# The second pass of the attention's scores with a stationary operand of 128 rows

## The chip, the cores and the metric

The kernel runs on one core of a Trainium2 chip. The metric is the device time of one execution in microseconds. The engines named below are TensorE (PE; its weight loads are listed apart as PEld), VectorE (DVE), ScalarE (ACT), GpSimd (POOL) and SyncE (SP), which issues the transfers.

## The reference

One layer of a decoder trunk over 2048 tokens of width 1024, all in float32: a normalised input is projected for three groups of heads (a state-space group, a gated linear recurrence, and an attention with forget gates), their outputs are projected back, a gated feed-forward of width 2816 follows, and then a gated embedding term. The change touches the attention alone. For one head with queries q and keys k of 64 elements, and cum, the running sum of the logarithms of the forget gates, the reference computes

```python
logits = jnp.einsum("bqhe,bkhe->bhqk", q[:, q0:q1], k[:, :q1]).astype(jnp.float32) * scale
logits = logits + cum[:, :, q0:q1, None] - cum[:, :, None, :q1]
mask = (q0 + jnp.arange(Q_BLOCK))[:, None] >= jnp.arange(q1)[None, :]
logits = jnp.where(mask[None, None], logits, -jnp.inf)
probs = jax.nn.softmax(logits, axis=-1).astype(v.dtype)
outs.append(jnp.einsum("bhqk,bkhe->bqhe", probs, v[:, :q1]))
```

There are 6 such heads.

## The kernel before

TensorE multiplies in a format (fp32r) that holds fewer bits than float32. So every factor x is split into a high part, which is x rounded to that format, and a low part, which is the rest. A product is made of three passes into one bank of the accumulator: high x high, high x low, low x high (lines 190 to 192 for all projections, each with 128 rows of contraction and 512 tokens).

The tokens go in 4 blocks of 512. Phase 1 projects the input and writes q, k and v to DRAM in both parts; phase 1b holds the state-space group, with the attention of token block 0 among it; phase 3 holds the feed-forward of each token block, with the attention of the next block put in small pieces between the products (`Side.tick`, called from `mm3`). The attention of block qc handles one head after another: `scores(h)` is a run of pieces, each one query block of 128 (line 560, `qi`) against up to 512 keys (line 568, `kc`), and `outputs(h)` transposes the probabilities and multiplies them with the values (lines 602 to 608). A tile scheduler sets the final order of the instructions on each engine from priorities and a timeline model; on the chip each engine then works through its list in that order.

For the scores a head has 64 elements, so both parts of a factor fit into 128 partitions. `qx` holds the high part of q in partitions 0 to 63 and the low part in 64 to 127; `kx` holds the low part of k in 0 to 63 and the high part in 64 to 127. One pass of 128 rows (line 571) thus gives q high x k low + q low x k high. The second pass (line 572) gives q high x k high: for it `qh` repeats the high part of q in partitions 64 to 127, where the high part of k lies, and both operands are the upper 64 partitions alone.

The tiles `qx`, `kx`, `qh` and `cum` have one buffer each. The transfers for the next head are issued from SP's queue once the last score of a head has read them. The scores go to four accumulator banks in turn (`xa`, `xe`, `xb`, `xc`). DVE adds the running sums and takes the row's maximum on the way out (line 576); ACT applies the exponential (line 583); DVE divides by the row's sum (line 586).

Of the kernel before, what the change touches and what calls it, by code (L numbers as in the profile page):

```python
# [19 lines left out]
P = 128  # L20
# [12 lines left out]

# columns of the packed parameters, one value per partition
PC = {}
# [5 lines left out]
NPC = _n  # L41
NALL = PC["scw"]  # of these the first are used all along


class Side:
    """work put in small pieces between the products of the main line"""

# [17 lines left out]
class Trunk:  # L65
# [17 lines left out]

    # ---------------------------------------------------------------- pieces
    def consts(self):
# [14 lines left out]
    def softplus(self, x, n):  # L100
        """log(1 + exp(x)) on a small tile, log1p by its atanh series (argument at most 1/3)."""
        nc, p = self.nc, self.spool
# [27 lines left out]
    def rms(self, ssq, n, tag="xc"):  # L130
        """1/sqrt(mean + eps) of every token, on all partitions (PSUM)."""
        nc = self.nc
        ms = self.ps(tag, (P, NCH))
        for c in range(NCH):
            nc.tensor.matmul(ms[:, c:c + 1], lhsT=ssq[:, c * P:(c + 1) * P], rhs=self.ones[:, 0:1], start=True, stop=True)
        v = self.t(self.small, [P, NCH], "rv")
        nc.vector.tensor_scalar(v, ms, 1.0 / n, EPS, op0=ALU.mult, op1=ALU.add)
        r = self.t(self.small, [P, NCH], "rr")
        nc.gpsimd.tensor_tensor(r, v, self.mhalf, op=ALU.pow)
        rh = self.t(self.small, [P, NCH], "rh", F32R)  # L140
        nc.vector.tensor_copy(rh, r)
        rl = self.t(self.small, [P, NCH], "rl")
        nc.vector.tensor_tensor(rl, r, rh.bitcast(F32), op=ALU.subtract)
        rb = self.ps(tag)
        for i, x in enumerate((rh.bitcast(F32), rl)):
            dg = self.t(self.tmp, [P, TB], "sq", F32R, bufs=3)
            nc.vector.tensor_tensor(dg.rearrange("p (a b) -> p a b", a=NCH), self.ident.unsqueeze(1).to_broadcast([P, NCH, P]),
                                    x.unsqueeze(2).to_broadcast([P, NCH, P]), op=ALU.mult)
            nc.tensor.matmul(rb, lhsT=self.onesr, rhs=dg, start=i == 0, stop=i == 1)
        return rb  # L150
# [13 lines left out]
    def split(self, hi, lo, x, g):  # L164
        """hi + lo = x * g in two tiles of the tensor engine's precision."""
        nc = self.nc
# [6 lines left out]
    def weight(self, src, nk):  # L173
        """A block of weights from DRAM in two parts, hi and lo: [P, 2, nk, P]."""
        nc = self.nc
# [7 lines left out]
    def mm3(self, w, u, rate=0):  # L183
        """w^T u in three passes; u: list of [P, 2, TB]; rate: pieces of the side work to put between"""
        nc = self.nc
# [10 lines left out]
    def parts(self, k, x, eng):  # L196
        """x as hi + lo"""
        nc = self.nc
# [5 lines left out]
    def norm_split(self, h, g, inplace=False, eng=None, tag="mm"):  # L204
        """RMSNorm of h [P, KD, TB] with gain, as a list of hi/lo tiles"""
        nc = self.nc
# [8 lines left out]
    def norm_store(self, blocks, n, row, tb, tag="xc"):  # L215
        """normalised (gain still missing) blocks of the mixer's output to DRAM"""
        nc = self.nc
# [6 lines left out]

    # ---------------------------------------------------------------- phase 1
    def load_norm(self, tb, xp):
# [9 lines left out]
    def phase1(self, ctx):  # L236
        """norm, v, forget gates and steps, LRU, q, k"""
        nc, tc, a = self.nc, self.tc, self.a
# [4 lines left out]
        u_next = self.load_norm(0, one)  # L243
        # block diagonal weights of the LRU gates
        self.load_mpar(one)
# [26 lines left out]
        for tb in range(NTB):  # L272
# [5 lines left out]
            if tb == 0:  # L278
                # weights of v, f and dt stay
                wv = self.t(one, [P, 2, KD, 396], "wv", F32R)  # L280
# [9 lines left out]
    def qk(self, nm, b, tb, u, two):  # L290
        """two heads of q (scaled) or k, in two parts, to DRAM"""
        nc = self.nc
# [8 lines left out]
    def values(self, tb, u, wv, sgn, mul, two):  # L301
        """v of the attention, f and dt, token-major; running sums of log f and of a dt within chunks"""
        nc = self.nc
# [33 lines left out]
    def lru(self, tb, u, wa, halo, hba, msp, carry, two):  # L337
# [16 lines left out]
        for b in range(2):  # L354
            tg = []
            for g in range(2):
# [4 lines left out]
                tg.append(th)  # L361
            # t = tanh(log(a) / 2), expm1(log a) = 2 t / (1 - t)
            tt = tg[0]
# [19 lines left out]
    def phase1b(self, ctx):  # L383
        """SSD"""
        nc, tc, a = self.nc, self.tc, self.a
# [11 lines left out]
        for tb in range(NTB):  # L397
# [13 lines left out]
            if tb == NTB - 1:  # L411
                # the first tokens of the next phase
                yx = self.load_y(0)
# [15 lines left out]
    def conv(self, wsrc, u, halo, cw, cb, two, dst, silu):  # L429
        """projection of one block of channels, causal convolution over 4 tokens; with silu the taps come halved"""  # L430
        nc = self.nc
# [16 lines left out]
    def ssd_chunk(self, tb, c, xbc, small, state, ys, two):  # L448
# [5 lines left out]
        acol = small[:, 1, c]  # L454
        # running sums along the chunk on all partitions
        ab = self.t(two, [P, 6, P], "ab")
        nc.sync.dma_start(ab, self.drow[tb, c * 12 + 6:c * 12 + 12].partition_broadcast(P))
        # token-major x and B
        ptr = self.ps("xa", (P, 3, P))
# [8 lines left out]
        nc.scalar.activation(bt, pgb[:, 2:4], ACT.Copy)  # L468
        # decays: of the whole chunk, to its end, from its start
        ex = self.t(two, [P, 3, 6], "ex")  # L470
# [9 lines left out]
        nc.scalar.activation(seg, seg, ACT.Exp)  # L480
        # x * dt, and the same decayed to the end of the chunk
        px = ptr.rearrange("p j (i e) -> p (j i) e", i=2)
# [4 lines left out]
        for g in range(2):  # L487
            nc.vector.tensor_tensor(seg[:, 3 * g:3 * g + 3], seg[:, 3 * g:3 * g + 3],
                                    pgb[:, g].unsqueeze(1).to_broadcast([P, 3, P]), op=ALU.mult)
        # token-major y from the state before the chunk and from the chunk itself  # L490
        yt = self.t(two, [P, 6, 64], "yt", bufs=1)
        if not first:
# [3 lines left out]
            nc.vector.tensor_tensor(yt, pso, ex[:, 2].unsqueeze(2).to_broadcast([P, 6, 64]), op=ALU.mult)  # L496
        # state at the end of the chunk
        pst = self.ps("xa", (P, 6, 64))
# [21 lines left out]

    # ---------------------------------------------------------------- phase 2
    def att_setup(self):
        """negated running sums of log f over all tokens, one head per partition; the mask of a diagonal block"""
        nc = self.nc
# [13 lines left out]
    def attention(self, qc, pool, tags, tag_o):  # L538
        """forgetting attention of one block of queries; a generator that yields between small pieces"""
        nc = self.nc  # L540
# [5 lines left out]
        def scores(h):  # L546
# [6 lines left out]
            for s in range(2):  # L553
                nc.sync.dma_start(qx[64 * s:64 * s + 64].bitcast(F32), q[:, s])
                nc.sync.dma_start(kx[64 - 64 * s:128 - 64 * s].bitcast(F32).rearrange("p a b -> p (a b)"), k[:, s])
            nc.sync.dma_start(qh[64:128].bitcast(F32), q[:, 0])
            nc.sync.dma_start(cum.rearrange("p a b -> p (a b)"), self.dcum[h, 0:n * TB].partition_broadcast(P))
            probs = []
            for qi in range(NCH):
# [7 lines left out]
                for kc in range(n):  # L567
# [3 lines left out]
                    nc.tensor.matmul(ps[:, :w], lhsT=qx[:, qs], rhs=kx[:, kc, :w], start=True, stop=False)  # L571
                    nc.tensor.matmul(ps[:, :w], lhsT=qh[64:128, qs], rhs=kx[64:128, kc, :w], start=False, stop=True)  # L572
                    d = w - P if k1 == W else w
# [47 lines left out]

    # ---------------------------------------------------------------- phase 3
    def load(self, src):
# [4 lines left out]
    def load_y(self, tb):  # L628
        """the mixer's output with gains; the rest of the attention's part is done before it is normalised here"""
        nc = self.nc  # L630
# [15 lines left out]
    def mix(self, tb, c, yx):  # L646
        """a block of columns of the mixer's projection and the residual"""
        x = self.load(self.a["xt"][c, :, tb * TB:(tb + 1) * TB])
# [5 lines left out]
    def phase3(self, ctx):  # L654
# [10 lines left out]
        for tb in range(NTB):  # L665
# [3 lines left out]
            if more:  # L669
                side.start(self.attention(tb + 1, one, ("xa", "xe", "xb", "xc"), "xd"))  # L670
                # pieces of attention for each block of columns
                rate = 6 * (8 * (tb + 2) + 1) / RATE
# [18 lines left out]
            u = self.norm_split(h, "g3", eng=V, tag="xe")  # L691
            # the embedding's projection
            px = self.t(one, [P, 4, TB], "kx", F32R)
# [9 lines left out]
            for c in range(KD):  # L703
# [3 lines left out]
                nc.scalar.activation(em[c], ps, ACT.Copy)  # L707
            # the gate, among the first products of the next tokens
            hn = []
# [43 lines left out]
def layout(inp):  # L753
    f = {k: np.asarray(v) for k, v in inp.items()}
    A = np.ascontiguousarray

    def blocks(w):  # [K, C] -> [C/128, 128 (k inner), K/128, 128 (c)]
        k, c = w.shape
        return A(w.reshape(k // P, P, c // P, P).transpose(2, 1, 0, 3))

    def cols(v):  # [n*128] -> [128, n]
        return v.reshape(-1, P).T
# [47 lines left out]
```

## Time and profile before

| what | value |
|---|---|
| median of 3 runs | 3008.57 us (3006.9 to 3009.61) |
| span of the profiled execution | 3008.8 us |
| PE busy | 2902.0 us (96%) |
| DVE, ACT, POOL busy | 1755.2, 1175.0, 1211.1 us |
| first score pass, line 571 | 240 matmuls |
| second score pass, line 572 | 240 matmuls |
| three passes of the projections, lines 190 to 192 | 1306.9, 1294.3, 1292.9 us busy |

Busy time of TensorE is the union of modelled spans that overlap: a matmul of 512 columns is listed with some 400 ns, and the next one starts before it ends. What a matmul occupies of the engine is read from the distance between starts. The profiled execution lies within 0.3 us of the median of the runs, so its numbers can be used for the runs as they stand.

### The profile page before, as it was taken

The numbers are of one execution on the slowest core, as the hardware profiler recorded it, in microseconds if no ns is written. First come the engines' busy times: TensorE is split into PE (matmuls) and PEld (weight loads), VectorE is DVE, ScalarE is ACT, GpSimd is POOL, SyncE is SP. The second block draws the span as 40 slices with busy tenths as digits, with TensorE's granted clock in tenths as the row PEclk, the third lists the DMA queues.
The fourth block names the chain that finished last, engine by engine and source line by source line (L and its number), as shares of the span: only waits on it lengthen the run. The fifth ranks groups of instructions, "written<-read, shape, count | busy, mean of one in ns | idle before, by whom it ended". The sixth has DMA issues, their size and how long they took to land.

```text
span 3008.8 us, 34985 instructions
## 1 busy us (share of the span) xinstructions
PE 2902.0 (96%) x12981; PEld 2307.3 (77%) x12981; DVE 1755.2 (58%) x3001; ACT 1175.0 (39%) x1751; POOL 1211.1 (40%) x635
## 2 busy tenths in 40 slices
PE   6998899999999999999999999999999999999997
PEld 5777677777877778877777788777777888788885
DVE  7888768988654533646555446564564464623246
ACT  5454434443343333434333334343343343322233
POOL 5444555333433334443233344433223344444442
PEclk9999999998999999999999999999999999999998
DMA  5444444343433333433343334243333243332331
GB/s 181 167 160 155 158 144 151 115 153 108 154 119 107 124 101 108 144 109 124 111 132 100 120 108 145 84 145 105 113 117 109 71 127 123 113 98 94 101 96 67
DMA packets 154301, 365.46 MB, mean 121 GB/s; under 512 B 17260, under 2 KB 48652, under 8 KB 152588
## 3 DMA queue, kind: packets, MB, share of 16 engines
q1 hardware_dynamic: 154130, 363.21, 37.3%
q8 instruction: 103, 1.69, 0.2%
q14 instruction: 68, 0.56, 0.1%
HBM read 318.87 MB, written 44.29 MB: 121 GB/s over the span
## 4 chain that ended last, share of the span: by engine, by line
PE 75%; DVE 14%; DMA 3%; ACT 3%; issue 3%; POOL 1%; SPq 0%; POOLq 0%; DVEq 0%; ACTq 0%
PE mm L190 21%; PE mm L191 21%; PE mm L192 21%; PE xd L608 1%; PE xd L607 1%; DVE xbc L440 1%; DVE h L440 1%; DVE u L201 1%; DMA ld<-dy 1%; DVE seg L479 1%; PE xa L602 1%; PE xa L572 1%; PE xb L572 1%; PE xe L602 1%; POOL w L180 1%
## 5 line engine op out<-in xcount | busy, mean ns | idle before, releaser
L180 POOL TENSOR_TENSOR w<-wst,w 128x1024 fp32r<-128x1024 f32 (+1 forms) x424 | 1029.4, 2429 | 1437.6 <-ACT w L179 1353.5
L190 PE MATMUL mm<-u,w 128*128 128x512 f32 x3264 | 1306.9, 402 | 11.9 <-ACT u L200 7.8
L191 PE MATMUL mm<-u,w 128*128 128x512 f32 x3264 | 1294.3, 397 | 11.9 <-DVE u L201 11.8
L192 PE MATMUL mm<-u,w 128*128 128x512 f32 x3264 | 1292.9, 397 | 0.5 <-POOL w L180 0.5
L190 PEld LDWEIGHTS mm<-u,w 128*128 128x128 f32 x3264 | 618.4, 190 | 159.0 <-issue 21.5
L191 PEld LDWEIGHTS mm<-u,w 128*128 128x128 f32 x3264 | 619.2, 190 | 145.1 <-DVE u L201 16.4
L192 PEld LDWEIGHTS mm<-u,w 128*128 128x128 f32 x3264 | 618.7, 190 | 134.4 <-issue 8.2
L179 ACT ACTIVATE w<-wst 128x1024 fp32r<-128x1024 f32 (+1 forms) x424 | 440.4, 1040 | 549.6 <-PE mm L192 354.3
L684 DVE SCALAR_TENSOR_TENSOR u<-th,u 128x512 fp32r<-128x512 f32 x88 | 187.8, 2134 | 59.8 <-ACT u L683 59.5
L583 ACT ACTIVATE lg<-lg,m 128x128 f32<-128x128 f32 (+7 forms) x96 | 115.4, 1202 | 181.7 <-DVE m L581 175.1
L161 DVE TENSOR_TENSOR ssq<-ssq,sq 128x512 f32<-128x512 f32 x111 | 133.6, 1203 | 57.2 <-ACT sq L157 55.2
L681 DVE TENSOR_TENSOR th<-th,mm 128x512 f32<-128x512 f32 x88 | 60.3, 685 | 172.0 <-PE mm L192 171.3
L690 DVE TENSOR_TENSOR h<-h,mm 128x512 f32<-128x512 f32 x96 | 65.5, 685 | 133.8 <-PE mm L192 133.3
L679 ACT ACTIVATE th<-mm 128x512 f32<-128x512 f32 x88 | 52.6, 597 | 228.9 <-PE mm L192 228.7
L563 POOL TENSOR_TENSOR cd<-cum,maskT 128x128 f32<-128x128 f32 x96 | 47.6, 496 | 202.9 <-DVE mx L576 117.6
L680 DVE SCALAR_TENSOR_TENSOR th<-th,mm 128x512 f32<-128x512 f32 x88 | 60.2, 685 | 117.6 <-ACT th L679 117.6
L718 DVE SCALAR_TENSOR_TENSOR th<-th,lg 128x512 f32<-128x512 f32 x32 | 31.0, 968 | 111.4 <-ACT th L717 111.3
L586 DVE TENSOR_SCALAR lg<-lg,r 128x128 f32<-128x128 f32 (+7 forms) x96 | 94.1, 981 | 2.6
L608 PE MATMUL xd<-ph,vc 128*128 128x512 f32 x216 | 83.6, 390 | 0.0
L607 PE MATMUL xd<-ph,vc 128*128 128x512 f32 x216 | 81.0, 375 | 0.0
L606 DVE TENSOR_TENSOR ph<-xa,ph 128x512 fp32r<-128x512 f32 x54 | 37.2, 688 | 50.9 <-ACT ph L605 50.7
L606 DVE TENSOR_TENSOR ph<-xc,ph 128x512 fp32r<-128x512 f32 (+1 forms) x66 | 36.6, 555 | 47.3 <-ACT ph L605 47.3
(293 smaller groups left out, 3228.8 us busy)
## 6 DMA issues: line engine op xcount, KB each, us to landing
wst<-in_w_gate SPq DMA_DIRECT2D x88, 512.0 KB, 3.5
wst<-in_w_up SPq DMA_DIRECT2D x88, 512.0 KB, 3.5
wst<-in_w_down SPq DMA_DIRECT2D x64, 448.0 KB, 3.3
wst<-in_w_out SPq DMA_DIRECT2D x32, 512.0 KB, 3.6
wst<-in_w_down SPq DMA_DIRECT2D x32, 512.0 KB, 3.5
wst<-in_w_pg SPq DMA_DIRECT2D x32, 512.0 KB, 3.5
vc<-dv SPq DMA_DIRECT2D x60, 256.0 KB, 3.6
wst<-in_w_xbc SPq DMA_DIRECT2D x28, 512.0 KB, 3.5
```

The costliest lines, as they stand in the source:

```text
L161: (eng or nc.gpsimd).tensor_tensor(acc, acc, s, op=ALU.add)
L179: nc.scalar.activation(w[:, 0], st, ACT.Copy)
L180: nc.gpsimd.tensor_tensor(w[:, 1], st, w[:, 0].bitcast(F32), op=ALU.subtract)
L190: nc.tensor.matmul(ps, lhsT=w[:, 0, k], rhs=x[:, 0], start=k == 0, stop=False)
L191: nc.tensor.matmul(ps, lhsT=w[:, 0, k], rhs=x[:, 1], start=False, stop=False)
L192: nc.tensor.matmul(ps, lhsT=w[:, 1, k], rhs=x[:, 0], start=False, stop=k == n - 1)
L583: nc.scalar.activation(lg, lg, ACT.Exp, bias=m, scale=1.0, accum_out=l)
L586: nc.vector.tensor_scalar(lg, lg, r, None, op0=ALU.mult)
L606: nc.vector.tensor_tensor(ph[:, 1, sl], pt[:, sl], ph[:, 0, sl].bitcast(F32), op=ALU.subtract)
L607: nc.tensor.matmul(po[:, sl], lhsT=vc[:, kt], rhs=ph[:, 0, sl], start=kt == 0, stop=False)
L608: nc.tensor.matmul(po[:, sl], lhsT=vc[:, kt], rhs=ph[:, 1, sl], start=False, stop=kt == nkt - 1)
L684: nc.vector.scalar_tensor_tensor(hh[:, 1], th, 0.5, hh[:, 0].bitcast(F32), op0=ALU.mult, op1=ALU.subtract)
```

## The change

`qh` gets all 128 partitions: the high part of q in 64 to 127, as before, and now the low part in 0 to 63. The second pass multiplies the whole of `qh` with the whole of `kx` and so gives q high x k high + q low x k low. The fourth product of the parts, low x low, which was left out before, comes with it. For this there is one more transfer of 64 partitions per head. Comments and documentation lines are dropped as well (not shown); since one line is added, lines from 557 on have a number higher by one.

```diff
-            nc.sync.dma_start(qh[64:128].bitcast(F32), q[:, 0])
+            for s in range(2):
+                nc.sync.dma_start(qh[64 - 64 * s:128 - 64 * s].bitcast(F32), q[:, s])
...
                     nc.tensor.matmul(ps[:, :w], lhsT=qx[:, qs], rhs=kx[:, kc, :w], start=True, stop=False)
-                    nc.tensor.matmul(ps[:, :w], lhsT=qh[64:128, qs], rhs=kx[64:128, kc, :w], start=False, stop=True)
+                    nc.tensor.matmul(ps[:, :w], lhsT=qh[:, qs], rhs=kx[:, kc, :w], start=False, stop=True)
```

The scheduler's lists for the two kernels are the same but for a few places. On SP's queue, this is the start of a head of token block 3 before (dq, dk, dcum and dv are the scratch tensors in DRAM, wst the staging of a weight block):

```order
L554 DMA qx_11599<-dq_81 64x512
L555 DMA kx_11597<-dk_82 64x1536
L554 DMA qx_11599<-dq_81 64x512
L555 DMA kx_11597<-dk_82 64x1536
L556 DMA qh_11600<-dq_81 64x512
L557 DMA cum_11598<-dcum_88 128x1536
L177 DMA wst_11881<-in_w_gate 128x1024
```

and now:

```order
L554 DMA qx_11612<-dq_81 64x512
L555 DMA kx_11610<-dk_82 64x1536
L554 DMA qx_11612<-dq_81 64x512
L555 DMA kx_11610<-dk_82 64x1536
L557 DMA qh_11613<-dq_81 64x512 x2
L558 DMA cum_11611<-dcum_88 128x1536
L177 DMA wst_11895<-in_w_gate 128x1024
```

The second transfer into `qh` stands right behind the first; `cum` and all that follows is one place further back. It is the same at each of the 24 heads.

On TensorE the order differs by more than a place or two only in phase 1b, around the last heads of token block 0. There the end of one head's outputs (xe) and the first scores of the next head (xc, xd) stood here before (mm are the products of a projection):

```order
L608 MATMUL xe_4826<-ph_4882,vc_4824 128x256
L607 MATMUL xe_4826<-ph_4898,vc_4824 128x128
L608 MATMUL xe_4826<-ph_4898,vc_4824 128x128
L571 MATMUL xc_4954<-kx_4940,qx_4942 128x128
L572 MATMUL xc_4954<-kx_4940,qh_4943 128x128
L571 MATMUL xd_4978<-kx_4940,qx_4942 128x256
L572 MATMUL xd_4978<-kx_4940,qh_4943 128x256
L190 MATMUL mm_5906<-u_1237_5770,w_5903 128x512
```

and now stand here:

```order
L190 MATMUL mm_5954<-u_1237_5776,w_5951 128x512
L191 MATMUL mm_5954<-u_1237_5776,w_5951 128x512
L609 MATMUL xe_4831<-ph_4887,vc_4829 128x256
L608 MATMUL xe_4831<-ph_4903,vc_4829 128x128
L609 MATMUL xe_4831<-ph_4903,vc_4829 128x128
L572 MATMUL xc_4960<-kx_4945,qx_4947 128x128
L573 MATMUL xc_4960<-kx_4945,qh_4948 128x128
L572 MATMUL xd_4984<-kx_4945,qx_4947 128x256
L573 MATMUL xd_4984<-kx_4945,qh_4948 128x256
L516 MATMUL xb_5431<-ident_91,yt_5412 128x128 x3
```

They have moved behind most of the next projection (mm_5954 is the one that follows mm_5912, the old mm_5906), some 20 products later in TensorE's list. In phase 3 the difference is a handful of single places.

## The prediction

> **What bounds the kernel now.** I read the page first (its busy times and its chain), then the busy times by stretch, then the matmuls one by one where the changed line stands.
>
> ```profile
> span 3008.8 us, 34985 instructions
> PE 2902.0 (96%) x12981; PEld 2307.3 (77%) x12981; DVE 1755.2 (58%) x3001; ACT 1175.0 (39%) x1751; POOL 1211.1 (40%) x635
> PE 75%; DVE 14%; DMA 3%; ACT 3%; issue 3%; POOL 1%; SPq 0%; POOLq 0%; DVEq 0%; ACTq 0%
> ...
> L192 PE MATMUL mm<-u,w 128*128 128x512 f32 x3264 | 1292.9, 397 | 0.5 <-POOL w L180 0.5
> ```
>
> TensorE is busy nearly all the time and makes up three quarters of the chain that ended last. The last row shows that weights are never late: the third pass waited for GpSimd's low parts for 0.5 us in the whole run. By stretch (the first two are the phases ahead of the feed-forward, the next three hold the attention of token blocks 1 to 3, the last has no attention):
>
> ```profile
> 400.00:670.00 270.00, 254.33 (x1238) 202.97 (x1238) 230.59 (x515) 119.79 (x220) 127.05 (x85) 0.99 0.45 145
> 670.00:1240.00 570.00, 561.42 (x2537) 447.32 (x2536) 311.69 (x580) 207.41 (x319) 219.31 (x119) 0.99 0.37 119
> 1240.00:1830.00 590.00, 586.63 (x2609) 457.80 (x2608) 312.16 (x542) 229.81 (x328) 221.58 (x115) 1.00 0.37 118
> 1830.00:2410.00 580.00, 578.88 (x2564) 443.39 (x2564) 311.64 (x575) 228.42 (x316) 199.66 (x103) 0.99 0.35 109
> 2410.00:3009.00 599.00, 574.92 (x2523) 472.58 (x2521) 269.36 (x288) 194.42 (x260) 251.53 (x110) 0.98 0.31 102
> ```
>
> Columns are stretch, length, then busy time of PE, weight loads, DVE, ACT, POOL, then granted clock, DMA share, GB/s. From 670 to 2410 us TensorE idles 8.6 + 3.4 + 1.1 = 13 us in 1740, while DVE is at 54%. So whatever time a matmul gives up there comes off the end. From 400 to 670 us DVE is at 85% and TensorE at 94%: two engines share the bound.
>
> But a busy TensorE need not be streaming. The group by line for the second score pass (64 rows) shows that something holds it:
>
> ```profile
> L572 PE MATMUL xa<-kx,qh x54: 439/497/503, 824.0 to 2331.0; 64*128 64x512 f32 x48, 64*128 64x384 f32 x6
> ...
>   issue: 69.6, 215
> ```
>
> Its weight loads follow 69.6 us of idle load time in 215 places, in which nothing was waited for. What that is, the matmuls in order of time show (start, duration; durations overlap, so starts are what to subtract):
>
> ```profile
> 1984.16 0.40 PE L571 MATMUL xa<-kx,qx 128*128 128x512 f32 x1
> 1984.49 0.50 PE L572 MATMUL xa<-kx,qh 64*128 64x512 f32 x1
> 1984.91 0.50 PE L190 MATMUL mm<-u,w 128*128 128x512 f32 x1
> 1985.25 0.40 PE L571 MATMUL xe<-kx,qx 128*128 128x512 f32 x1
> 1985.58 0.49 PE L572 MATMUL xe<-kx,qh 64*128 64x512 f32 x1
> 1986.00 0.50 PE L191 MATMUL mm<-u,w 128*128 128x512 f32 x1
> 1986.34 0.40 PE L571 MATMUL xc<-kx,qx 128*128 128x512 f32 x1
> 1986.66 0.50 PE L572 MATMUL xc<-kx,qh 64*128 64x512 f32 x1
> 1987.09 0.50 PE L192 MATMUL mm<-u,w 128*128 128x512 f32 x1
> 1987.43 0.40 PE L190 MATMUL mm<-u,w 128*128 128x512 f32 x1
> 1987.66 0.39 PE L191 MATMUL mm<-u,w 128*128 128x512 f32 x1
> ...
> 1989.95 0.40 PE L571 MATMUL xb<-kx,qx 128*128 128x512 f32 x1
> ```
>
> Two full-row matmuls follow each other at 1987.66 - 1987.43 = 0.23 us. Around a 64-row one the steps are 0.33 (1984.16 to 1984.49), 0.42 and 0.34, that is 1.09 us for three matmuls in place of 0.69. **Each 64-row pass costs 0.40 us beyond a full-row one.** The weight loads say why:
>
> ```profile
> 1984.48 0.18 PEld L572 LDWEIGHTS xa<-kx,qh 64*128 64x128 f32 x1 [0.37 <-issue]
> 1984.91 0.19 PEld L190 LDWEIGHTS mm<-u,w 128*128 128x128 f32 x1 [0.25 <-issue]
> 1985.02 0.19 PEld L571 LDWEIGHTS xe<-kx,qx 128*128 128x128 f32 x1
> ```
>
> The load for 1985.25 starts at 1985.02, a matmul ahead of its use. The load of the 64-row operand starts only with its own matmul (1984.48 and 1984.49), and so does the load of the full-row operand behind it (1984.91). Twice per pair a load of about 0.19 us is not hidden, which is 0.38 of the 0.40.
>
> **The change part by part.** (1) The second pass gets 128 rows. It streams the same columns (0.23 us for 512), its load is as long (0.18 against 0.19), and there is no other shape left beside it. Line 572 is the one score pass of 64 rows; by the loops it runs 6 heads x 4 query blocks x (1 + 2 + 3 + 4) = 240 times, 24 of them ahead of 670 us and 216 behind. Of each head's pieces in token block qc, 4 qc + 1 are 512 wide and one each is 384, 256 and 128 wide, so of the 216 there are 162 of full width and 54 narrower. For the narrowest I take this place:
>
> ```profile
> 1387.48 0.22 PE L571 MATMUL xb<-kx,qx 128*128 128x128 f32 x1
> 1387.63 0.32 PE L572 MATMUL xb<-kx,qh 64*128 64x128 f32 x1
> ...
> 1388.22 0.40 PE L192 MATMUL mm<-u,w 128*128 128x512 f32 x1
> ```
>
> From 1387.48 to 1388.22 are 0.74 us for two narrow and one wide matmul. Full-row, the wide one takes 0.23; for each narrow one the bounds are a quarter of that (0.06) and a load's length (0.19), so the excess lies between 0.74 - 0.61 = 0.13 and 0.74 - 0.35 = 0.39. I take 0.3. For 384 and 256 columns, which lie between, I take 0.38. Sum behind 670 us: 162 x 0.40 + 18 x 0.38 x 2 + 18 x 0.3 = 64.8 + 13.7 + 5.4 = 84 us. TensorE is the bound there, so I count all but 3 us of it, for waits that today's slower pace covers: 81 us.
>
> Ahead of 670 us stand 24 pieces, 6 of each width: 6 x (0.40 + 0.38 + 0.38 + 0.3) = 9 us. With DVE at 85% there, it may be worth between 9 and, as the order of the attention's products among those of the state-space part moves by some 20 products, a loss of 5. I take the middle of 0 and 9, 5 us with rounding.
>
> (2) What uncovers after that? A score's bank must be free before its next use, and DVE frees it:
>
> ```profile
> 1983.47 0.69 DVE L576 CUSTOM_DVE_ANT_0 lg<-xb,cum 128x512 f32<-128x512 f32 x1 [1.18 <-PE xb L572]
> ...
> 1985.02 0.69 DVE L576 CUSTOM_DVE_ANT_0 lg<-xa,cum 128x512 f32<-128x512 f32 x1 [0.67 <-PE xa L572]
> 1985.64 0.08 DVE L576 DVE_READ_ACCUMULATOR2_ANT mx<- 128x1 f32 x1
> ...
> 1989.69 0.69 DVE L681 TENSOR_TENSOR th<-th,mm 128x512 f32<-128x512 f32 x1 [0.45 <-PE mm L192]
> ```
>
> Bank xb is read out by 1984.16 and written next at 1989.95, 5.8 us later; and DVE waits for TensorE (0.67 us), not the other way. That covers the 0.4 us by which a piece gets shorter.
>
> (3) One more transfer per head, 24 in all, of 64 partitions (128 KB). It stands on SP's queue right behind the first transfer into qh; behind it wait the running sums (cum), then weight blocks and values.
>
> ```profile
> 817.51 0.59 SPq L556 DMA_DIRECT2D qh<-dq  x1
> ...
> 1998.27 0.59 SPq L556 DMA_DIRECT2D qh<-dq  x1
> ...
> DMA to landing us min/median/max: 2.9/5.3/8.9
> ```
>
> ```profile
> 824.00 0.50 PE L572 MATMUL xa<-kx,qh 64*128 64x512 f32 x1
> ...
> 2033.70 0.50 PE L572 MATMUL xa<-kx,qh 64*128 64x512 f32 x1
> ```
>
> An issue takes 0.59 us. In the usual case (1998.27) the operand is used 35 us later, while the head before is multiplied with its values; the second transfer lands in 0.59 + 8.9 us at most. Only the first head of block 1 is tight: issue 817.51, use 824.00, 6.5 us, and 0.59 + 5.3 = 5.9 just fits. Cost: 0, and 24 x 0.59 = 14 us if that cover were gone at every head. DVE, ACT and POOL get no instruction more.
>
> **Sum**, against the profiled execution: 3008.8 - 81 - 5 = 2923 us. Its span is within 0.3 us of the median of the runs (3008.57), so nothing is added: **2923 us**.
>
> **The rivals.** *DVE paces the bursts.* Pieces come in bursts of about four. After the change one takes 0.69 us of TensorE against 0.69 + 0.08 - overlap, about 0.70 us, of DVE (1985.02 to 1985.72). If a main-line operation (0.69, line 681) falls into each burst and the bank's cover is used up, 216 / 4 x 0.69 = 37 us come back: 2960 us. Against it: the 5.8 us of cover and a DVE at 54%. I give it 10%.
>
> *The rows are not the reason.* The load of 64 rows takes 0.18 us against 0.19, so by duration alone nothing is gained, and it would be 3009 us, no change. The trace speaks against it: loads start late around this shape and nowhere else in the bursts. I give it 3%. The Trainium skill ("TensorE: Matmul & The Clock Gate", LDWEIGHTS (loading the stationary operand)) says that a load's time goes by columns and that the row count doesn't matter; by that rule alone the sum would be this rival's. The rows 0.18 and 0.19 agree with it, but it says nothing of when the load may start. The skill's "TensorEngine Tiling (Array Packing)", Key Properties, says that a change of tiling mode drains the engine; by that rule the sum is my own.
>
> *Slower: the head starts late.* With qh landing after the head's turn, TensorE stands at line 573 with the main line's products queued behind it. It decides from 86 / 24 = 3.6 us per head on; with the issue and the longest landing fully exposed, 0.59 + 8.9 = 9.5 us, it would be 3009 - 86 + 24 x 9.5 = 3151 us. At 35 us of cover in the usual head I give it 2%. A fall of the granted clock would have to reach 5% (86 of 1740 us), and the last stretch, all full-row passes, has 0.98.
>
> **How the numbers follow.** My forecast has 83%, the three rivals 10, 3 and 2, and 2% go to gains beyond the range. Low end: all 84 and 9 us and some luck of the new order, 2910. High end: the early phase loses 5 instead of gaining, 10 us less, and half of the DVE rival's 37 us come back, 2951. This kernel's measurement tells some 0.2% (6 us) from no change. Faster: 83 + 10 + 2 = 95%; within: 3%; slower: 2%.
>
> **What would show it.** Right: steps of 0.23 us between lines 572, 573 (the old 571, 572) and the next matmul; loads of line 573 a matmul ahead, its idle "issue" time near 0; TensorE's weight loads unchanged in number; the stretch with 96 pieces shorter by about 37 us, and the last stretch unchanged. Wrong: the steps stay at 0.33 and 0.42 (the second rival); idle time before lines 572 or 190 released by DVE (the first); or by a landing of qh or cum (the third).

## The result, and the profile after

The changed kernel takes 2930.56 us (median of 4 runs, 2927.95 to 2933.44) against 3009.09 us beside it: a ratio of 0.9738 with a 95% interval of 0.9724 to 0.9752, 78.5 us less. Forecast were 2923 us, 2910 to 2951.

The page of the changed kernel, its totals and its chain of waits:

```profile
span 2926.6 us, 35034 instructions
PE 2812.5 (96%) x12981; PEld 2317.3 (79%) x12981; DVE 1751.9 (60%) x3001; ACT 1175.7 (40%) x1751; POOL 1213.2 (41%) x635
...
PE 72%; DVE 3%; issue 1%; DMA 1%; ACT 1%; POOL 0%; POOLq 0%; DVEq 0%; ACTq 0%
```

The numbers of matmuls and weight loads are as before, and so is the work of the other engines. TensorE's busy time fell by 89.5 us, the span by 82.2. (The shares of the chain add up to 78% here and to 99% before, so they can't be compared one by one.) By stretch (columns as before; the bounds lie where the same work starts and ends now, about):

```profile
400.00:670.00 270.00, 252.42 (x1253) 206.57 (x1253) 230.97 (x511) 121.21 (x221) 126.26 (x85) 0.98 0.46 148
670.00:1220.00 550.00, 539.21 (x2512) 445.42 (x2511) 310.04 (x584) 206.09 (x318) 218.69 (x119) 0.98 0.39 124
1220.00:1780.00 560.00, 555.65 (x2594) 458.34 (x2593) 310.53 (x540) 227.34 (x325) 220.84 (x114) 1.00 0.39 125
1780.00:2330.00 550.00, 546.69 (x2607) 452.37 (x2606) 310.61 (x577) 231.84 (x322) 204.59 (x104) 1.00 0.38 119
2330.00:2927.00 597.00, 572.62 (x2506) 470.80 (x2504) 268.27 (x287) 193.86 (x260) 250.46 (x109) 0.98 0.30 102
```

In the three stretches with attention TensorE still has few gaps (18 us in 1660, where it was 13 in 1740), and VectorE is at 56%. The second score pass (now line 573), by line, and in order of time in a burst of the last attention block:

```profile
L573 PE MATMUL xa<-kx,qh x54: 335/392/403, 824.5 to 2248.5; 128*128 128x512 f32 x48, 128*128 128x384 f32 x6
```

```profile
1929.40 0.40 PE L190 MATMUL mm<-u,w 128*128 128x512 f32 x1
1929.64 0.39 PE L572 MATMUL xa<-kx,qx 128*128 128x512 f32 x1
1929.87 0.40 PE L573 MATMUL xa<-kx,qh 128*128 128x512 f32 x1
1930.10 0.39 PE L191 MATMUL mm<-u,w 128*128 128x512 f32 x1
1930.33 0.40 PE L572 MATMUL xe<-kx,qx 128*128 128x512 f32 x1
```

```profile
1929.40 0.19 PEld L572 LDWEIGHTS xa<-kx,qx 128*128 128x128 f32 x1
1929.64 0.19 PEld L573 LDWEIGHTS xa<-kx,qh 128*128 128x128 f32 x1
1929.87 0.19 PEld L191 LDWEIGHTS mm<-u,w 128*128 128x128 f32 x1
```

Every step is 0.23 us now; from one first pass to the next (1929.64 to 1930.33) it is 0.69 us, where it was 1.09. Each load starts a matmul ahead of its use, and the idle time under "issue" is gone from the line's group. The whole trace says the same: before, 239 of the 240 loads for the second pass start no more than 2 ns ahead of their matmul, and the loads for the matmuls behind them no more than 3 ns; now the median load for the second pass starts 227 ns ahead.

Where in the program did the time go? One instruction, the same in all traces (the 3015th matmul), serves as a mark near the end of the early phases: a matmul of line 192 right behind a state-space chunk's transposes of line 466. All 24 pieces of block 0 lie ahead of it and all others behind it. It stands here before

```profile
733.13 0.48 PE L192 MATMUL mm<-u,w 128*128 128x512 f32 x1
```

and here after

```profile
733.32 0.48 PE L192 MATMUL mm<-u,w 128*128 128x512 f32 x1
```

Up to this mark nothing was gained. Behind it, 3008.8 - 733.1 = 2275.7 us became 2926.6 - 733.3 = 2193.3 us: the whole 82 us. The two stretches behind the mark, before and after (columns as above):

```profile
733.13:3008.80 2275.67, 2246.12 (x9970) 1775.40 (x9968) 1148.09 (x1854) 832.88 (x1173) 876.37 (x435) 0.99 0.35 113
```

```profile
733.32:2926.60 2193.28, 2160.81 (x9970) 1783.04 (x9968) 1142.46 (x1854) 833.10 (x1173) 877.71 (x435) 0.99 0.37 118
```

TensorE's busy time fell by 85.3 us there, and its idle time rose by 2.9 us (29.6 to 32.5).

### The profile page after: what moved, and what is told of

It is laid out like the page before. It is cut to its first block, busy times and chain, and to the rows that moved or that the text cites. A ratio compares the mean times of both kernels' runs of the same rounds, so it can differ in the third digit from the quotient of the medians.

```text
span 2926.6 us, 35034 instructions
## 1 busy us (share of the span) xinstructions
PE 2812.5 (96%) x12981; PEld 2317.3 (79%) x12981; DVE 1751.9 (60%) x3001; ACT 1175.7 (40%) x1751; POOL 1213.2 (41%) x635
## 4 chain that ended last, share of the span: by engine, by line
PE 72%; DVE 3%; issue 1%; DMA 1%; ACT 1%; POOL 0%; POOLq 0%; DVEq 0%; ACTq 0%
PE mm L191 20%; PE mm L192 20%; PE mm L190 20%; PE xd L609 2%; PE xd L608 2%; PE xa L603 1%; DMA ld<-dy 1%; PE xe L603 1%; PE xb L603 1%; PE xc L603 1%; PE xa L572 0%; PE xa L573 0%; DVE th L719 0%; DVE u L168 0%; PE xb L573 0%
## 5 line engine op out<-in xcount | busy, mean ns | idle before, releaser
L139 POOL TENSOR_TENSOR rr<-rv,mhalf 128x4 f32<-128x4 f32 x28 | 29.1, 1041 | 88.1 <-DVE rv L137 75.3
```

## The experiments

In the texts on record "the change" is the changed kernel, and "before" the kernel before. All ratios below are to the kernel before on the same chip, with 95% intervals.

**Where the 64 rows lie.** The theory is that a pass of 64 rows among full ones costs, as the loads on both sides of it come late. A rival is the place: the operand starts at partition 64.

```diff
-                nc.sync.dma_start(qx[64 * s:64 * s + 64].bitcast(F32), q[:, s])
-                nc.sync.dma_start(kx[64 - 64 * s:128 - 64 * s]...
-            nc.sync.dma_start(qh[64:128].bitcast(F32), q[:, 0])
+                nc.sync.dma_start(qx[64 - 64 * s:128 - 64 * s].bitcast(F32), q[:, s])
+                nc.sync.dma_start(kx[64 * s:64 * s + 64]...
+            nc.sync.dma_start(qh[0:64].bitcast(F32), q[:, 0])
...
-                    nc.tensor.matmul(..., lhsT=qh[64:128, qs], rhs=kx[64:128, kc, :w], ...)
+                    nc.tensor.matmul(..., lhsT=qh[0:64, qs], rhs=kx[0:64, kc, :w], ...)
```

> The second pass still has 64 rows, but they lie in partitions 0 to 63 (the halves of kx and qx are swapped, qh holds the high part of q in 0 to 63); TensorE's order is the one of before. If the 0.40 us per piece come from a pass of fewer rows among full ones: no change, 3009 us (within 6), steps around the 64-row pass of 0.33, 0.42 and 0.34 us. If they come from where the rows start (partition 64): as after the change, 2925 to 2935 us, steps of 0.23.

Measured: 3010.52 us, ratio 1.0 (0.999 to 1.0011). The matmuls in order of time:

```profile
1984.32 0.40 PE L571 MATMUL xa<-kx,qx 128*128 128x512 f32 x1
1984.65 0.50 PE L572 MATMUL xa<-kx,qh 64*128 64x512 f32 x1
1985.08 0.50 PE L190 MATMUL mm<-u,w 128*128 128x512 f32 x1
1985.41 0.40 PE L571 MATMUL xe<-kx,qx 128*128 128x512 f32 x1
```

Steps of 0.33, 0.43 and 0.33 us, 1.09 in all, as before. The place is not the reason.

**96 rows.** Does every pass of fewer than 128 rows pay?

```diff
+            nc.sync.dma_start(qh[64:96].bitcast(F32), q[0:32, 1])
...
-                    nc.tensor.matmul(..., lhsT=qh[0:64, qs], rhs=kx[0:64, kc, :w], ...)
+                    nc.tensor.matmul(..., lhsT=qh[0:96, qs], rhs=kx[0:96, kc, :w], ...)
```

(on top of the kernel with the low half)

> The second pass has 96 rows (partitions 0 to 95, halves swapped as in the other kernel with the low half): high x high and half of low x low, with one more transfer of 32 partitions per head. If every pass of fewer than 128 rows pays: 3009 us. If only a pass that fits into half of the rows pays, because the array is then used in another mode: 2925 to 2935 us, with loads a matmul ahead.

Measured: 2933.99 us, ratio 0.9748 (0.9725 to 0.9772).

```profile
1941.11 0.39 PE L572 MATMUL xa<-kx,qx 128*128 128x512 f32 x1
1941.33 0.39 PE L573 MATMUL xa<-kx,qh 96*128 96x512 f32 x1
1941.56 0.40 PE L191 MATMUL mm<-u,w 128*128 128x512 f32 x1
1941.80 0.39 PE L572 MATMUL xe<-kx,qx 128*128 128x512 f32 x1
```

0.69 us for the three, as with 128 rows. So it is not the count as such: 96 rows cost nothing, 64 rows cost 0.40 us. The Trainium skill ("TensorEngine Tiling (Array Packing)", Tiling Modes) lists 128, 64 and 32 rows as the modes of the array, and says under Key Properties that changing the mode drains it; 96 rows are not on that list, and it is my reading that they fall under the 128-row mode. The runs with 64, 96 and 128 rows agree with that reading. In all, the span behind the mark is 2194.0 us here, as after the change; the mark itself comes late, at 740.3.

**Grouping the 64-row passes.** If the change between the two shapes costs, two 64-row passes in a row should pay once.

```diff
+                made = []
...
-                    ps = self.ps(next(banks))
-                    nc.tensor.matmul(ps[:, :w], lhsT=qx[:, qs], rhs=kx[:, kc, :w], start=True, stop=False)
-                    nc.tensor.matmul(ps[:, :w], lhsT=qh[64:128, qs], rhs=kx[64:128, kc, :w], start=False, stop=True)
+                    if kc % 2 == 0:
+                        made = [(c, self.ps(next(banks)), min(W, (c + 1) * TB) - c * TB) for c in range(kc, min(kc + 2, n))]
+                        for c, ps, v in made:
+                            nc.tensor.matmul(ps[:, :v], lhsT=qx[:, qs], rhs=kx[:, c, :v], start=True, stop=False)
+                        for c, ps, v in made:
+                            nc.tensor.matmul(ps[:, :v], lhsT=qh[64:128, qs], rhs=kx[64:128, c, :v], start=False, stop=True)
+                    ps = made[kc % 2][1]
```

> Passes stay at 64 rows, but the two passes of two neighbouring key blocks are issued in the order first, first, second, second, so that 64-row passes follow each other. In the scheduler's list the 240 of them then form 201 runs, against 239 before: 38 passes of 64 rows stand behind another one. If what costs is the change between 64 and 128 rows: 38 x 0.40 = 15 us less, 2994 us, and the load of the second 64-row pass is a matmul ahead. If each 64-row load is late whatever stands before it, only the late load behind it is saved: 38 x 0.20 = 8 us less, 3001 us. If grouping does nothing: 3009 us.

Measured: 2992.58 us, ratio 0.9946 (0.9933 to 0.9958), 16 us less, which is the 15 us of the theory and twice the 8 us of its rival. The total alone is a weak judge: in the profiled execution, the slowest of the five, the span behind the mark is 2262.4 us, 10 to 13 less than in the kernels with single 64-row passes. The loads decide. A group in order of time, and two of its loads (line 574 is the first pass here, 576 the second):

```profile
2172.47 0.39 PE L574 MATMUL xb<-kx,qx 128*128 128x512 f32 x1
2172.70 0.28 PE L574 MATMUL xc<-kx,qx 128*128 128x256 f32 x1
2172.90 0.49 PE L576 MATMUL xb<-kx,qh 64*128 64x512 f32 x1
2173.24 0.28 PE L576 MATMUL xc<-kx,qh 64*128 64x256 f32 x1
2173.44 0.50 PE L192 MATMUL mm<-u,w 128*128 128x512 f32 x1
2173.78 0.40 PE L190 MATMUL mm<-u,w 128*128 128x512 f32 x1
```

```profile
2172.90 0.18 PEld L576 LDWEIGHTS xb<-kx,qh 64*128 64x128 f32 x1 [0.24 <-issue]
2173.01 0.19 PEld L576 LDWEIGHTS xc<-kx,qh 64*128 64x128 f32 x1
2173.44 0.19 PEld L192 LDWEIGHTS mm<-u,w 128*128 128x128 f32 x1 [0.25 <-issue]
```

The first 64-row load is late and so is the full-row load behind the group. The one between them starts at 2173.01, well ahead of its matmul at 2173.24. It is so in the whole trace: the loads of all 39 passes that follow another 64-row pass start 226 to 236 ns ahead of their matmuls, those of the other 201 at most 2 ns. Three matmuls of 512 columns and two of 256 take 1.31 us (2172.47 to 2173.78), where 3 x 0.23 + 2 x 0.12 = 0.93 would do (0.12 us is the median step behind 256 columns among full-row passes): 0.38 us for one way in and out with two passes inside.

**The rows without the transfer.** The low half of `qh` is zero, set once per block; the products are the three of before, the transfers are those of before, and so is TensorE's order.

```diff
+        qh = self.t(pool, [P, TB], "qh", F32R)
+        nc.gpsimd.memset(qh[0:64].bitcast(F32), 0.0)
...
-                    nc.tensor.matmul(..., lhsT=qh[64:128, qs], rhs=kx[64:128, kc, :w], ...)
+                    nc.tensor.matmul(..., lhsT=qh[:, qs], rhs=kx[:, kc, :w], ...)
```

> The second pass has 128 rows, but the low half of qh is zero (set once per block of queries by GpSimd) and nothing more is transferred; it computes the three products of before, and TensorE's order is the one of before. If the row count alone gains: 3009 - 78 = 2931 us (2925 to 2935), as after the change. If the extra transfers or the moved order cost something in the change, this is faster than it by that: down to 2922 us, the missing 9 us of the early phase. If the gain depended on what is multiplied, it would be off the change's time by more than 10 us.

Measured: 2926.57 us, ratio 0.9723 (0.9708 to 0.9738). The row count alone gives all of the gain. The 9 us of the early phase don't show here either: its mark stands at

```profile
732.21 0.48 PE L192 MATMUL mm<-u,w 128*128 128x512 f32 x1
```

0.9 us ahead of the kernel before, with the order of before. (A second trace of this kernel, further down, has it at 729.6: one mark is good to some 3 us.)

**The transfer without the rows.** The changed kernel, its second pass back on the upper 64 rows.

```diff
             for s in range(2):
                 nc.sync.dma_start(qh[64 - 64 * s:128 - 64 * s].bitcast(F32), q[:, s])
...
-                    nc.tensor.matmul(..., lhsT=qh[:, qs], rhs=kx[:, kc, :w], ...)
+                    nc.tensor.matmul(..., lhsT=qh[64:128, qs], rhs=kx[64:128, kc, :w], ...)
```

> The extra transfer into qh of the change, while the second pass stays at the upper 64 rows. If transfers are hidden, as predicted: no change, 3009 us (within 4). If they cost an issue of 0.59 us per head on the path: 3009 + 14 = 3023 us. If the change's scheduler order alone were what gains: 2930 us.

Measured: 3013.55 us, ratio 1.0014 (1.0004 to 1.0023): 4 us slower, neither nothing nor 14. The order alone gains nothing. The mark of the early phase:

```profile
737.99 0.48 PE L192 MATMUL mm<-u,w 128*128 128x512 f32 x1
```

It comes 4.9 us later than before; the two traces that there are of one kernel differ by 1.7 and 2.7 us (the change, zero low half). Behind it are 3012.4 - 738.0 = 2274.4 us against 2275.7: in phase 3 the transfers of 18 heads cost nothing. The 4 us are lost in the early phase, by its six transfers or by the order, which the scheduler moved there; this run doesn't tell which.

**Block 0 alone, and blocks 1 to 3 alone.**

```diff
+                    r0 = 0 if qc == 0 else 64
+                    nc.tensor.matmul(ps[:, :w], lhsT=qh[r0:128, qs], rhs=kx[r0:128, kc, :w], start=False, stop=True)
```

(and the low half transferred where it is used; in the other kernel the condition is `qc > 0`)

> The change in the attention of token block 0 alone (24 of 240 pieces, among the state-space part); blocks 1 to 3 stay at 64 rows. If VectorE holds the early phase, as the two traces suggest: no change, 3009 us (within 4). If the early phase gained the 5 us of my prediction: 3004 us; all 9 us: 3000 us.

Measured: 3012.86 us, ratio 1.0009 (1.0 to 1.0018). The 24 pieces of the early phase gain nothing, together with their transfers and the moved order.

> The change in the attention of token blocks 1 to 3 alone (216 of 240 pieces). If all of the gain comes from there: 2931 us (within 4), as after the change. If the early phase takes part with 5 to 9 us: 2936 to 2940 us.

Measured: 2929.37 us, ratio 0.9734 (0.972 to 0.9747). The 216 pieces behind the mark gain it all.

**Relief of VectorE in the early phase.** If VectorE hides the gain there, less work on it should bring the gain out.

```diff
-        nc.vector.tensor_copy(raw[:, 0:3], halo)
+        if silu:
+            nc.scalar.activation(raw[:, 0:3], halo, ACT.Copy)
...
-        nc.vector.tensor_copy(halo, raw[:, TB:TB + 3])
+        if silu:
+            nc.scalar.activation(halo, raw[:, TB:TB + 3], ACT.Copy)
```

(elsewhere the copies stay) on the changed kernel,

> The change, and beside it the two small copies per convolution of the state-space part (3 columns each, lines 434 and 438) go from VectorE to ScalarE: 28 x (0.41 + 0.33) = 21 us less of VectorE between 330 and 690 us. If VectorE holds the early phase and hides the change's gain there: below the change's time, by up to 9 us from the 24 pieces and more from the copies themselves, 2905 to 2922 us. If VectorE doesn't hold it: as the change, 2931 us.

on the kernel before,

> The same relief of VectorE on the kernel before. If VectorE holds the early phase: 2990 to 3003 us, and the distance to the change with the same relief is larger than the 78 us of the medians, up to 87. If TensorE's switches hold it as much: 3009 us, and the distance stays 78.

and the changed kernel again beside them.

> The changed kernel once more, on the same chip as the two kernels with the relief, so that they are compared with it there: 2931 us (within 4).

Measured: 2920.49 us with the change (ratio 0.9706, 0.9692 to 0.9719), 3006.42 us without it (0.9993, 0.9984 to 1.0002), and 2930.0 us for the change as it is (0.9738, 0.9724 to 0.9751). So the relief is worth 9.5 us on the changed kernel and 2 us on the one before, where the interval includes none. The kernel before thus met neither forecast, though the distance of the two, 86 us, is close to the 87 of the theory. But the relief also moves TensorE's order: up to the mark its list differs from the one without the relief in at least fifty places, on the kernel before as on the changed one. So the 9.5 us are not VectorE's time alone. With the relief the two kernels have the same list up to the mark but for one product. The next run has the list of the relief on the kernel before, instruction for instruction on TensorE:

> 128 rows with the zero low half (no transfer added) and the relief of VectorE by the two small copies together; TensorE's order is the one of the relief on the kernel before. If the moved order cost the change its 4 us and the relief gives what it gave there (9 us), this is the fastest: 2915 to 2920 us. If the early phase is held by something else than VectorE: 2926 us, as without the relief. Against the relief on the kernel before (3006 us), the early phase (up to the first products of the feed-forward) should gain more than the 1 us that it gains without the relief, up to 9 us, if VectorE is what hides it.

> 128 rows with the zero low half once more, on the same chip as the one with the relief: 2927 us (within 4).

Measured: 2921.32 us (0.9706, 0.9692 to 0.972), between the two forecasts, and 2927.59 us (0.973, 0.9716 to 0.9744; 2922.81 to 2932.19) without the relief. The kernel is among the two fastest. But its early phase shows no gain from the rows: the mark stands at

```profile
729.28 0.50 PE L192 MATMUL mm<-u,w 128*128 128x512 f32 x1
```

with 128 rows and at

```profile
728.39 0.50 PE L192 MATMUL mm<-u,w 128*128 128x512 f32 x1
```

with 64, both with the relief. By the medians the rows are worth 85 to 86 us with the relief and 79 to 83 without it, and 82 of that lie behind the mark; so a few of the missing 9 us may have come out, no more than these runs can tell. One thing the relief does settle in part: with it, the change (six more transfers in the early phase) and the zero low half (none) have the same order but for one product, and they take 2920.49 and 2921.32 us. There the transfers cost nothing, so the 4 us above point to the moved order.

The relief was also smaller than I had reckoned: VectorE's busy time from 330 to 726 us, before and with the relief on the kernel before, is

```profile
330.00:726.00 396.00, 363.79 (x1721) 291.52 (x1720) 333.07 (x729) 169.51 (x305) 165.78 (x104) 0.96 0.41 133
```

```profile
330.00:726.00 396.00, 368.24 (x1747) 297.42 (x1748) 327.58 (x681) 177.03 (x363) 166.87 (x105) 0.95 0.41 133
```

5.5 us less, not 21. The means that I had multiplied, 0.41 and 0.33 us, come from a few long entries; the median copy takes 0.17 us (minimum, median and maximum in ns stand behind the counts):

```profile
L434 DVE COPY raw<-halo x36: 143/169/2344, 1.3 to 687.1; 128x3 f32<-128x3 f32 x36
```

```profile
L438 DVE COPY halo<-raw x36: 149/166/1257, 36.6 to 691.0; 128x3 f32<-128x3 f32 x36
```

The test was too weak to decide.

| kernel | median us | mark of the early phase | TensorE idle, 400 us to mark | span behind it |
|---|---|---|---|---|
| 64 rows in all blocks: before | 3009.09 | 733.1 | 23.1 | 2275.7 |
| the same, low half | 3010.52 | 733.0 | 19.5 | 2272.5 |
| the same, transfer alone | 3013.55 | 738.0 | 24.0 | 2274.4 |
| the same, relief on before | 3006.42 | 728.4 | 19.8 | 2274.9 |
| the same, grouped | 2992.58 | 733.4 | 22.3 | 2262.4 |
| 128 rows in block 0 alone | 3012.86 | 737.3 | 30.3 | 2273.9 |
| 128 rows in blocks 1 to 3 alone | 2929.37 | 731.2 | 19.3 | 2193.8 |
| 128 rows in all blocks: the change | 2930.56 | 733.3 | 27.5 | 2193.3 |
| the same, once more | 2930.0 | 735.0 | 27.2 | 2190.8 |
| the same, zero low half | 2926.57 | 732.2 | 24.2 | 2191.0 |
| the same, zero low half once more | 2927.59 | 729.6 | 24.2 | 2191.4 |
| the same, zero low half and relief | 2921.32 | 729.3 | 24.2 | 2192.4 |
| the same, the change and relief | 2920.49 | 726.0 | 24.7 | 2192.0 |
| 96 rows in all blocks | 2933.99 | 740.3 | 28.9 | 2194.0 |

(The mark is the start of the same product of line 192 in each trace, the span behind it the trace's span less the mark. Medians are of all runs of a kernel, the marks of one profiled execution. The kernel before took 3008.57 to 3010.11 us beside them.) But for the grouped kernel the last column has two values, 2272.5 to 2275.7 and 2190.8 to 2194.0, by the rows of the second pass in blocks 1 to 3 and by nothing else.

## Why the prediction was right, and where it was off

- *What bounds the kernel.* Right for phase 3: the gain there is 82 us on average in the table, where the sum had 84 and I counted 81. Both parts of that came as forecast: TensorE's busy time behind the mark fell by 85.3 us, and 2.9 us of it, where I had kept back 3, went into waits that the slower pace had covered. From the first to the last second pass the three blocks took 271.2, 337.4 and 408.6 us before and 253.7, 311.2 and 369.2 after: 17.5, 26.2 and 39.4 us less for 48, 72 and 96 pieces. Behind the last one nothing changed (671.1 and 672.6 us).
- *0.40 us per 64-row pass.* Right, in size and in reason. The loads on both sides of the pass came late; with 128 rows they are a matmul ahead. That it is the change of shape, in and out, is now shown by the grouped kernel (0.38 us for a group of two), and that it is neither the place nor the mere count by the kernels with the low half and with 96 rows.
- *The early phase: 5 us.* **This term was mis-sized; it measured nothing**: the mark moved from 733.1 to 733.3 (735.0 in the second trace), and block 0 alone took 3012.86 us. The price of the 24 passes was not what failed. Added up over their places (the three steps from each first pass on, waits left out) the kernel with the zero low half, in the order of before, takes 9.0 us less than the kernel before. What failed is the share of it that reaches the mark. That kernel's mark comes at 729.6 and 732.2, and kernels with 64 rows there and the same order have it at 731.2 to 733.4: some 2 us, hardly more than the scatter. What came in its place is waiting. From 400 us to the mark, before and after:

```profile
400.00:733.13 333.13, 310.05 (x1497) 248.66 (x1497) 287.35 (x643) 146.97 (x269) 142.77 (x95) 0.96 0.41 133
```

```profile
400.00:733.32 333.32, 305.78 (x1497) 250.46 (x1497) 287.96 (x643) 147.24 (x269) 143.14 (x95) 0.95 0.42 135
```

  TensorE idles 27.5 us where it had idled 23.1, and of these 24.9 and 20.4 us end with an operation of VectorE. The table has the same for the other kernels: with 128 rows in block 0 TensorE idles 3 to 5 us more, on average, than with 64 rows in the same order. Another part is the moved order's. Towards the end of the phase, before and after:

```profile
691.12 0.50 PE L190 MATMUL mm<-u,w 128*128 128x512 f32 x1 [0.67 <-DVE t L423]
```

```profile
692.29 0.39 PE L609 MATMUL xe<-ph,vc 128*128 128x256 f32 x1 [1.37 <-DVE ph L607]
...
695.47 0.66 PE L190 MATMUL mm<-u,w 128*128 128x512 f32 x1 [2.40 <-DVE t L423]
695.93 0.63 PE L191 MATMUL mm<-u,w 128*128 128x512 f32 x1
696.35 0.63 PE L192 MATMUL mm<-u,w 128*128 128x512 f32 x1
...
699.22 0.39 PE L190 MATMUL mm<-u,w 128*128 128x512 f32 x1
699.45 0.39 PE L191 MATMUL mm<-u,w 128*128 128x512 f32 x1
```

  These two waits, 1.36 to 1.37 and 2.40 us, stand in all five traces with the moved order (the change twice, block 0 alone, 96 rows, and the transfer alone with its 64 rows), so they don't come from the rows. In the order of before the second one is 0 to 0.67 us with 64 rows and 0.92 or 0.93 with 128. That VectorE takes part of the gain is what these rows say; the relief didn't prove it, and the rest of the 9 us is not accounted for. I leave it open which of VectorE's operations, or what else, sets the mark.
- *The transfers cost nothing.* Right in phase 3, by the row on the transfer alone. In the early phase the transfers and the order that the scheduler moved with them cost some 4 us together; the pair with the relief and the two waits above point to the order.
- *The rivals.* VectorE did not pace the bursts: the last column holds no trace of 37 us. The rows were the reason. No head started late: behind the mark no wait of TensorE ended with the landing of a transfer.
- *What is left.* The forecast was 7.6 us too low. The sum was made for the span of one profiled execution, and that came out at 2926.6 instead of 2923: the 5 us of the early phase, less the 1.4 us by which phase 3 gained more than 81. Another 1.7 us are a step that the prediction left out: the run with that span took 2928.33 us, and every run on record takes 1.7 to 1.9 us longer than its span, so something had to be added to a span to make a run's time. The last 2.2 us are the distance of that run from the median of the four.

## What to carry to other kernels

Where TensorE is the bound, subtract the starts of neighbouring matmuls rather than trust its busy time: it was 96% busy with some 0.40 us lost at each of 240 places. A pass with 64 rows of contraction is not cheaper than one with 128; among full-row passes it costs a load of weights on its way in and one on its way out, so fill it up to 128 rows, with zeros if there is nothing better, or put such passes next to each other. And a gain counts only in those stretches where its engine is the bound: of 9 us that the passes gave up in the early phase, some 2 at most reached its end, and the moved order with its transfers took some 4.

## What the runs showed that I had not expected

A pass of 96 rows costs no more than one of 128 (steps of 0.22 to 0.24 us, 2194.0 us behind the mark).

The moved order cost TensorE pace as well. Behind the two waits above, its steps are 0.42 us (695.93 to 696.35) instead of 0.23, and by 699.22 they are 0.23 again; before, behind the shorter wait, they stayed at 0.23. In the stretches of 20 us before and after, the granted clock (the number behind the busy times) is

```profile
680.00:700.00 20.00, 17.44 (x85) 14.03 (x84) 19.31 (x34) 10.58 (x19) 5.30 (x3) 1.00 0.24 77
```

```profile
680.00:700.00 20.00, 16.23 (x72) 12.97 (x71) 18.90 (x33) 9.51 (x18) 5.36 (x3) 0.91 0.25 79
```

All five traces with the moved order have such steps behind the wait of 2.40 us. The transfer alone has them too, with 64 rows (from the fourth step on), so they don't come from TensorE's lead. What they cost can't be read off the whole phase: from 400 us to the mark the clock is 0.93 to 0.96 in all kernels, 0.96 before and 0.95 after. The Trainium skill ("TensorE: Matmul & The Clock Gate", What's actually happening) tells of a gate that lets through half of the clock after an idle window of some 3.4 us and all of it after a busy one. The steps of nearly double length for a little over 3 us agree with that; the two waits (1.37 and 2.40 us, with a few matmuls between) are each shorter than such a window, and no run here shows whether they add up.
